# Second gate as eight columns, and half of one expert's w1 in the place that this frees

## The chip, the cores and the metric

The kernel runs on one core of a Trainium2 chip. The metric is the device time of one execution in microseconds (us). Before the change it is 517.47 us, the median of three runs (516.98 to 517.79).

A core has five engines that run side by side, each through its own instructions in order: TensorE (PE in the profile; the loading of its stationary operand is PEld), VectorE (DVE), ScalarE (ACT), GpSimd (POOL) and SyncE (SP). All large loads are issued by SP, in one queue. 16 DMA engines move the data.

## The reference

One decoder layer over 256 tokens of 1024 features: a token mixer (retention and latent attention), and then a mixture of 32 experts in 4 groups, of which each token uses two of one group. Before both halves a vector `c` is turned by `w_ada` into shifts, scales and gates. What matters here is the last part and the second gate `g2`:

```
mod = silu(c) @ w_ada + b_ada
sh1, sc1, g1, sh2, sc2, g2 = split(mod, 6)
...
u = rmsnorm(h, norm2) * (1 + sc2) + sh2
h = h + g2 * hier_moe(u)          # 32 experts: (silu(u w1) * (u w3)) w2, weighted by the router
return rmsnorm(h, final_norm)
```

`w1` and `w3` of an expert are 1024 x 256 and `w2` is 256 x 1024, all float32: 1 MiB each, 96 MiB for the experts.

## The kernel before

The token mixer fills the first 300 us. Then comes the router (line 1426 on), and after it eight batches of four experts, batch `bt` with the experts 4 bt to 4 bt + 3. An expert takes at most 32 tokens, so the four experts of a batch make 128 rows. A batch is

- `hidden`: w1 and then w3 of its four experts, 64 + 64 products of 32 x 256 (`hidden_mm`, line 1418; w1 and w3 have 8 blocks k of 128 rows each),
- `gather` for the next batch: one-hot rows pick the tokens (line 1358), and four and four transposes (line 1369) turn them into `ug`,
- `expert_out`: w2 (line 1532), times the gate `g2b` (line 1535), and the sum into four accumulators (line 1541).

**Slots.** On-chip memory is cut into 27 slots of 128 partitions x 2048 floats, 1 MiB each (`Slots`). A load of a weight takes a whole slot, whatever it loads into it. Work tiles take slots as well: `ad["g"]` (the slot s20) holds, in its first half, first the gate g1 and later the gathered tokens `ug`, and in its second half `g2b`; `y` is the slot of batch results, taken after batch 0's `hidden`.

**Order of the loads.** `Loads` holds a fixed list: per batch four w1, four w3, four w2. Whenever a slot is taken or given back, `pump` issues the next loads of the list, as long as slots are free and a plan, made in a first dry pass, says that the work tiles will still find theirs. A slot that comes free goes to the end of a queue of free slots. On SP the loads then stand in that order, and each waits there for the last reader of what was in its slot; a load that waits holds up all loads behind it. In batch 0 w1 and w3 are loaded in quarters over four experts (`QB`), so that their eight slots come free one after the other as the products go on; in the other batches the four w1 slots come free together, then the four w3 slots and, at the end of `expert_out`, the four w2 slots.

**The second gate.** During the mixer VectorE adds up the products of `silu(c)` and the last sixth of `w_ada`, so that `g2b` holds partial sums per partition (part 5 of `ada2_task`). In the router `rows_of` (line 1043) sums them over the partitions and spreads the sum over all partitions in one step, in two halves: a product of a matrix of ones with 512 columns (line 1047), and a copy by ScalarE back into the same place (line 1048). The order of PE and DVE in the router is written out by hand; after it a scheduler orders the instructions of each engine.

Of the kernel before, what the change touches and what calls it, by code (L numbers as in the profile page):

```python
# [13 lines left out]
AF = mybir.ActivationFunctionType  # L14
# [16 lines left out]
QB = ("w1", 0), ("w3", 0), ("w3", 7)  # L31
# [21 lines left out]
FIRST = 4  # L53
RES_AT = 1
OVER_AT = 3

PACE_AT, PACE = 19, 2

# [149 lines left out]
def body(ctx, tc, A, out, plan=None):  # L208
    nc = tc.nc
    T, V, S, G, Q = nc.tensor, nc.vector, nc.scalar, nc.gpsimd, nc.sync  # L210
# [3 lines left out]
    SL = Slots(sp, NSLOT, 2048, "s")  # L214
    PB = Slots(pp, 8, 512, "b")
    LD = Loads(SL, plan)
    ring = Ring(SL)

    def bank(name="bank"):
        return PB.alloc(name)  # L220
# [26 lines left out]
    def ld(view, src):  # L247
        def fn(t):
            n = 1
            for d in src.shape[1:]:  # L250
                n *= d
            Q.dma_start(t[:, :n].rearrange(view[0], **view[1]) if view else t[:, :n], src)  # L252
        return fn

    def ld_k(src):

        return ld(("p (k n) -> p k n", dict(k=src.shape[1])), src)
# [43 lines left out]
    def ew(name, e):  # L301
        g, i = divmod(e, 8)
        k = 8 if name != "w2" else 2
        return A[name][0, g, i].rearrange("(p k) n -> p k n", k=k)
# [12 lines left out]
    def ld_quarter(name, b, kp):  # L317

        src = A[name][0, b // 2, b % 2 * 4:b % 2 * 4 + 4].rearrange("e (p c k) n -> p e c (k n)", c=4, k=2)
        return ld(("p (e n) -> p e n", dict(e=4)), src[:, :, kp])  # L320
# [5 lines left out]
    for b in range(8):  # L326
        for name in ("w1", "w3"):
            for j in range(4):
                LD.add((name, 4 * b + j), ld_quarter(name, b, j) if (name, b) in QB else ld_k(ew(name, 4 * b + j)))
            if (name, b) == ("w1", 7):  # L330
                LD.add("fn", ld_fn)
        for j in range(4):
            if b < 7:
                LD.add(("w2", 4 * b + j), ld_k(ew("w2", 4 * b + j)))
# [4 lines left out]
    cols2 = st.tile([128, 8], F32, name="n2c")  # L339
# [3 lines left out]
    ident = cst[:, C_ID:C_ID + 128]  # L343
    one = st.tile([128, 1], F32, name="one")
# [40 lines left out]
    def keep_warm(n, after=None):  # L385

        pb = bank()
        with tc.issue_after(after) if after is not None else ExitStack():
            for _ in range(n):
                T.matmul(pb.t, onesb, oneb[:, 0:1].to_broadcast([128, 512]), start=True, stop=True)  # L390
        pb.free()
# [83 lines left out]
    start = ExitStack()  # L475
# [4 lines left out]
    pb = bank()  # L480
# [7 lines left out]
    pb = bank()  # L488
# [155 lines left out]
    ad = {"g": SL.alloc("g12")}  # L644
# [398 lines left out]
    def rows_of(a, o, ns=range(2)):  # L1043

        for n in ns:
            pb = bank()
            T.matmul(pb.t, ones, a[:, n * 512:(n + 1) * 512], start=True, stop=True)
            S.activation(o[:, n * 512:(n + 1) * 512], pb.t, AF.Copy)
            pb.free()
# [144 lines left out]
    for i, u in enumerate(units):  # L1194
# [13 lines left out]
        if i + LOOK < len(units):  # L1208
            units[i + LOOK].prep()
            j, r = divmod(i - (i_y - PACE_AT), PACE)  # L1210
# [66 lines left out]
    def h_turned(b, w):  # L1277

        for i in range(8 // w):
            pb = bank()  # L1280
            for k in range(w):
                T.transpose(pb.t[:, k * 128:(k + 1) * 128], hp[:, b, w * i + k, :], ident)
            copy((V, S)[i % 2], ug[:, w * i:w * (i + 1), :], pb.t[:, :w * 128].rearrange("p (k t) -> p k t", k=w))
            pb.free()
# [48 lines left out]
    def ranks(b):  # L1333
        pb = bank()
        T.matmul(pb.t[:, 0:32], utri, Mb[:, b, :], start=True, stop=b == 0, skip_group_check=True)
        if b == 1:
            T.matmul(pb.t[:, 0:32], onesb, Mb[:, 0, :], start=False, stop=True, skip_group_check=True)
        V.scalar_tensor_tensor(rk1[:, b, :], pb.t[:, 0:32], 1.0, Mb[:, b, :], op0=ALU.add, op1=ALU.mult)
        pb.free()
# [3 lines left out]
    Sr = sml.rearrange("p (b s) -> p b s", b=2)  # L1343
    GT = rt_t.rearrange("p b n -> p (b n)")
    ht = wr.rearrange("p k n -> p (k n)")[:, 0:256]
    g2b = ad["g"].t[:, 1024:2048]
    ug = ad["g"].t[:, 0:1024].rearrange("p (k s) -> p k s", k=8)
    iota = cst[:, C_IOTA:C_IOTA + 32]

    def onehot(bt, b):  # L1350
        e4 = slice(4 * bt, 4 * bt + 4)
        V.tensor_tensor(S01[:, b], iota[:, None, :].to_broadcast([128, 4, 32]),
                        rk1[:, b, e4][:, :, None].to_broadcast([128, 4, 32]), ALU.is_equal)
        return V.tensor_scalar(Sr[:, b], S01[:, b].rearrange("p e s -> p (e s)"), rstd2[:, b:b + 1], None, op0=ALU.mult)  # L1354
# [42 lines left out]
    def gather(bt):  # L1397
        pg = [bank() for _ in range(2)]
        for b in range(2):
            onehot(bt, b)  # L1400
            gather_mm(pg, b)
        gather_out(pg, y_s.t[:, 1024:2048])
# [3 lines left out]
    def hidden_mm(bt, m, ks):  # L1406

        name = ("w1", "w3")[m]
        ph = ph_of[m]
        cut = (name, bt) in QB  # L1410
        for k in ks:
            c = k // 2 if cut else 0
            for j in range(4):
                if cut:
                    w = LD.get((name, 4 * bt + c)).t.rearrange("p (e k n) -> p e k n", e=4, k=2)[:, j, k % 2, :]
                else:
                    w = LD.get((name, 4 * bt + j)).t.rearrange("p (k n) -> p k n", k=8)[:, k, :]
                i = T.matmul(ph.t[32 * j:32 * j + 32, 0:256], ug[:, k, 32 * j:32 * j + 32], w,  # L1418
                             start=k == 0, stop=k == 7, skip_group_check=True, tile_position=(0, 32 * j))
            if cut and k % 2:  # L1420
                LD.done((name, 4 * bt + c))
            if cut and bt == 7 and k % 2:
                keep_warm(WARM7[m], i.ins)
        return i

    router = ExitStack()
    router.enter_context(tc.manual_schedule(engines={T.engine, V.engine}))
# [11 lines left out]
    hl_act["m"][1].free()  # L1439
    h_of(1)  # L1440
    ranks(0)
    rows_of(g2b, g2b, (0,))
    h_turned(1, 2)
    onehot(0, 0)
    h_rstd(1)
# [5 lines left out]
    keep_warm(WARM2)  # L1451
    ranks(1)
    onehot(0, 1)
    rows_of(g2b, g2b, (1,))
    keep_warm(WARM3)
    first_mm(pg, 1, range(FIRST))
    first_out(pg, range(FIRST))
    hidden_mm(0, 0, range(2))
    first_mm(pg, 1, range(FIRST, 8))
    last_v = first_out(pg, range(FIRST, 8)).ins  # L1460
# [6 lines left out]
    def combine_weights(bt):  # L1467
        e4 = slice(4 * bt, 4 * bt + 4)
        pb = bank()
        for b in range(2):  # L1470
            V.tensor_tensor(S01[:, b], S01[:, b], Gt[:, b, e4][:, :, None].to_broadcast([128, 4, 32]), ALU.mult)
            T.transpose(pb.t[:, b * 128:(b + 1) * 128], S01[:, b].rearrange("p e s -> p (e s)"), ident)
        S.activation(GT, pb.t[:, 0:256], AF.Copy)
        pb.free()
# [51 lines left out]
    def expert_out(bt, hdT):  # L1526
        py = [bank() for _ in range(2)]
        ts = [LD.get(("w2", 4 * bt + j)).t.rearrange("p (k n) -> p k n", k=2) for j in range(4)]
        for n in range(2):
            for k in range(2):  # L1530
                for j in range(4):
                    T.matmul(py[n].t[32 * j:32 * j + 32, :], hdT[:, k, 32 * j:32 * j + 32],  # L1532
                             ts[j][:, k, n * 512:(n + 1) * 512], start=k == 0, stop=k == 1, skip_group_check=True,
                             tile_position=(0, 32 * j))
            V.tensor_mul(y[:, n * 512:(n + 1) * 512], py[n].t, g2b[:, n * 512:(n + 1) * 512])
            py[n].free()
        for j in range(4):
            LD.done(("w2", 4 * bt + j))
        for b in range(2):
            for n in range(2):  # L1540
                T.matmul(fin[2 * b + n].t, GT[:, b * 128:(b + 1) * 128], y[:, n * 512:(n + 1) * 512], start=bt == 0,  # L1541
                         stop=bt == 7, skip_group_check=True)
# [61 lines left out]
    for bt in range(8):  # L1604
        if bt:
            combine_weights(bt)
        hdT = hidden(bt)
        if bt == 7:
            o_s = SL.alloc("out")
        if bt == 0:  # L1610
            fin = [bank("fin") for _ in range(4)]
            y_s = SL.alloc("y")
            y = y_s.t[:, 0:1024]
        if bt < 7:
            gather(bt + 1)
            expert_out(bt, hdT)
        if bt == RES_AT:

            for b in range(2):
                for n in range(2):  # L1620
                    f = fin[2 * b + n].t.rearrange("p (q k) -> p k q", k=8)
                    V.tensor_add(f, f, hp[:, b, :, n * 64:(n + 1) * 64])
        if bt == OVER_AT:
            overflow()
# [108 lines left out]
```

## Time and profile before

| | |
|---|---|
| median of 3 runs | 517.47 us |
| the profiled execution | 517.75 us, of which the profile's span is 516.0 us |
| PE busy | 488.7 us (95% of the span) |
| DVE, ACT, POOL busy | 283.1, 198.1, 61.4 us |
| moved by DMA | 174.86 MB, mean 339 GB/s |
| granted clock of TensorE | 0.99 of full speed |

The span runs from the first to the last instruction; the execution takes 1.75 us more. Matmuls are pipelined, and the profile's busy time of PE is not PE at its peak. A product of plain float32 shows as two weight loads and two matmuls, a transpose as one of each. The rows of the trace stand in their own section below. In the chain of waits the profile follows, back from the end, what released each instruction; a step called DMA there is a stretch in which a load was what was waited for.

### The profile page before, as it was taken

How to read it: one execution, taken by the hardware profiler on the slowest of the kernel's cores; microseconds unless marked ns; L12 is line 12 of the kernel's file. 1: busy time of each engine (PE TensorE's matmuls, PEld its weight loads, DVE VectorE, ACT ScalarE, POOL GpSimd, SP SyncE). 2: the span in 40 equal slices, each digit the busy share in tenths (PEclk: the TensorE clock that was granted, in tenths of full speed). 3: DMA queues.
4: the chain of work that ended last, by engine and by line, in shares of the span. 5: the costliest groups of instructions: out<-in, count | busy, mean ns of one | idle time of the engine just before them, and what ended most of it. 6: DMA issues, size and time to landing. Idle time of an engine off the chain costs nothing.

```text
span 516.0 us, 8592 instructions
## 1 busy us (share of the span) xinstructions
PE 488.7 (95%) x3432; PEld 339.0 (66%) x3435; DVE 283.1 (55%) x529; ACT 198.1 (38%) x366; POOL 61.4 (12%) x58
## 2 busy tenths in 40 slices
PE   6999999999999999999999999999999898969894
PEld 2778999997787878888888887443544434323332
DVE  2555789884696996984777746424333131302113
ACT  2545783453678444456534424202112020202013
POOL 1000321411000002105862000000000000000000
PEclk8999999999999999999999999999999999989998
DMA  9999999788967692899698898999999999999993
GB/s 270 324 318 358 314 339 399 304 305 309 358 229 267 207 362 84 304 373 382 243 370 325 313 360 293 417 406 422 415 420 418 415 422 415 419 421 417 393 330 113
DMA packets 68099, 174.86 MB, mean 339 GB/s; under 512 B 5423, under 2 KB 27092, under 8 KB 57817
## 3 DMA queue, kind: packets, MB, share of 16 engines
q1 hardware_dynamic: 65602, 174.01, 90.5%
q10 hardware_dynamic: 2454, 0.27, 0.4%
q8 instruction: 28, 0.46, 0.4%
q14 instruction: 15, 0.11, 0.1%
HBM read 173.22 MB, written 1.05 MB: 338 GB/s over the span
## 4 chain that ended last, share of the span: by engine, by line
PE 58%; DMA 27%; SPq 6%; DVE 4%; ACT 1%; issue 1%; POOL 1%; ACTq 1%; DVEq 0%; POOLq 0%
DMA s<-in_w 24%; PE b L381 10%; PE b L383 10%; PE b L382 10%; PE b L1418 5%; SPq L252 4%; SPq L244 2%; PE b L1532 2%; DMA s<-in_w_in 1%; PE b L1541 1%; PE b L1358 1%; PE b L535 1%; PE b L533 1%; PE b L534 1%; DVE s L467 1%
## 5 line engine op out<-in xcount | busy, mean ns | idle before, releaser
L467 DVE TENSOR_TENSOR s<-s,s 128x1024 fp32r<-128x1024 f32 (+2 forms) x92 | 103.5, 1136 | 43.9 <-ACT s L466 43.4
L466 ACT ACTIVATE s<-s 128x1024 fp32r<-128x1024 f32 (+2 forms) x92 | 83.5, 923 | 83.1 <-PE b L383 54.3
L381 PE MATMUL b<-s,s 128*128 128x512 f32 (+2 forms) x258 | 102.2, 396 | 1.0 <-ACT s L466 0.9
L383 PE MATMUL b<-s,s 128*128 128x512 f32 (+2 forms) x258 | 98.7, 383 | 0.0
L382 PE MATMUL b<-s,s 128*128 128x512 f32 (+2 forms) x258 | 98.1, 380 | 0.0
L1418 PE MATMUL b<-s,s 128*32 128x256 f32 x1024 | 62.3, 381 | 10.8 <-DMA s<-in_w 8.8
L381 PEld LDWEIGHTS b<-s,s 128*128 128x128 f32 x258 | 48.5, 188 | 15.6 <-ACT s L466 4.3
L1418 PEld LDWEIGHTS b<-s,s 128*32 128x32 f32 x1024 | 32.8, 110 | 38.5 <-DMA s<-in_w 11.9
L383 PEld LDWEIGHTS b<-s,s 128*128 128x128 f32 x258 | 48.4, 188 | 9.6 <-DVE s L467 0.4
L382 PEld LDWEIGHTS b<-s,s 128*128 128x128 f32 x258 | 48.6, 188 | 8.5 <-issue 0.2
L1064 DVE SCALAR_TENSOR_TENSOR s<-s,cs,s 128x1024 f32<-128x1024 f32 x32 | 41.4, 1292 | 0.3
L535 PE MATMUL b<-s,s 128*128 128x256 f32 x128 | 36.2, 284 | 0.4 <-DVE s L467 0.4
L533 PE MATMUL b<-s,s 128*128 128x256 f32 x128 | 36.4, 285 | 0.0
L534 PE MATMUL b<-s,s 128*128 128x256 f32 x128 | 36.2, 283 | 0.0
L1532 PE MATMUL b<-s,wr 128*32 128x512 f32 x224 | 34.1, 596 | 0.0
L377 DVE COPY s<-b 128x512 f32<-128x512 f32 (+2 forms) x13 | 8.1, 624 | 41.7 <-PE b L1358 29.0
L1358 PE MATMUL b<-s,sml 128*128 128x512 f32 x56 | 28.4, 639 | 0.2 <-DVE sml L1354 0.2
L375 ACT ACTIVATE s<-b 128x512 f32<-128x512 f32 (+2 forms) x25 | 14.1, 567 | 32.9 <-PE b L1358 18.3
L1541 PE MATMUL b<-s,rt 128*128 128x512 f32 x56 | 26.2, 611 | 0.0
L535 PEld LDWEIGHTS b<-s,s 128*128 128x128 f32 x128 | 24.4, 191 | 0.6 <-DVE s L467 0.6
L534 PEld LDWEIGHTS b<-s,s 128*128 128x128 f32 x128 | 24.4, 191 | 0.0
L533 PEld LDWEIGHTS b<-s,s 128*128 128x128 f32 x128 | 24.4, 191 | 0.0
(258 smaller groups left out, 631.6 us busy)
## 6 DMA issues: line engine op xcount, KB each, us to landing
s<-in_w SPq DMA_DIRECT2D x92, 1024.0 KB
s<-in_w_in SPq DMA_DIRECT2D x22, 1024.0 KB
s<-in_w_ada SPq DMA_DIRECT2D x16, 1024.0 KB
s<-in_w_ada SPq DMA_DIRECT2D x16, 512.0 KB
s<-in_w_mla_o SPq DMA_DIRECT2D x4, 1024.0 KB
s<-in_w_ret_o SPq DMA_DIRECT2D x4, 1024.0 KB
s<-in_w_out SPq DMA_DIRECT2D x4, 1024.0 KB
s<-in_w SPq DMA_DIRECT2D x6, 512.0 KB
```

The source lines that it names most:

```text
L381: T.matmul(o, l[0], r[0], start=start, stop=False, skip_group_check=True)
L382: T.matmul(o, l[1], r[0], start=False, stop=False, skip_group_check=True)
L383: return T.matmul(o, l[0], r[1], start=False, stop=stop, skip_group_check=True)
L466: S.activation(hi, src, AF.Copy)
L467: V.tensor_tensor(lo, src, hi, ALU.subtract)
L533: T.matmul(o, hi[:, f], mh, start=k == 0 and c == 0, stop=False, skip_group_check=True)
L534: T.matmul(o, hi[:, f], ml, start=False, stop=False, skip_group_check=True)
L535: T.matmul(o, lo[:, f], mh, start=False, stop=k == 7, skip_group_check=True)
L1064: V.scalar_tensor_tensor(a, t[:, kk, :], cs[:, k:k + 1], a, op0=ALU.mult, op1=ALU.add)
L1358: T.matmul(pg[k4].t, Sr[:, b], hp[:, b, 4 * k4:4 * k4 + 4, :].rearrange("p k q -> p (k q)"), start=b == 0, stop=b == 1, skip_group_check=True)
L1418: i = T.matmul(ph.t[32 * j:32 * j + 32, 0:256], ug[:, k, 32 * j:32 * j + 32], w, start=k == 0, stop=k == 7, skip_group_check=True, tile_po ...
L1532: T.matmul(py[n].t[32 * j:32 * j + 32, :], hdT[:, k, 32 * j:32 * j + 32], ts[j][:, k, n * 512:(n + 1) * 512], start=k == 0, stop=k == 1, s ...
```

## The change

Three edits:

- In the router `rows_of` is replaced by `g2_cols`: for each block k a product whose stationary operand is every eighth column of the partial sums (128 x 128) and whose moving operand is one column of ones. That gives g2 as 8 columns, which stand in `cols2`, a tile of 8 columns (in the trace n2c) whose earlier content is no longer read.
- The second half of s20 is then free. One load is added behind the second `g2_cols`: blocks 0 to 3 of w1 of expert 9 (`HALF`). The load of that expert's w1 in the list keeps its place and its slot, but loads only blocks 4 to 7.
- After `hidden` of batch 0 a new slot `g2` is taken, and `g2_rows` fills it: for each block k a product of column k, repeated 128 times as the stationary operand, with the identity, and after each four of them a ScalarE copy that writes with a stride of 8 floats. `expert_out` then reads `g2b` there as before, until the end.

```diff
+HALF = 9
@@ the list of loads
-                LD.add((name, 4 * b + j), ld_quarter(name, b, j) if (name, b) in QB else ld_k(ew(name, 4 * b + j)))
+                half = (name, 4 * b + j) == ("w1", HALF)
+                LD.add((name, 4 * b + j), ld_quarter(name, b, j) if (name, b) in QB else
+                       ld_k(ew(name, 4 * b + j)[:, 4 * half:, :]))
@@
-    g2b = ad["g"].t[:, 1024:2048]
+    gh = ad["g"].t[:, 1024:2048]
+    g2c = cols2
@@ hidden_mm
+                elif (name, 4 * bt + j) == ("w1", HALF):
+                    w = (LD.get((name, HALF)).t if k > 3 else gh).rearrange("p (k n) -> p k n", n=256)[:, k % 4, :]
@@
+    def g2_cols(ks):
+        pb = bank()
+        for k in ks:
+            T.matmul(pb.t[:, k:k + 1], gh[:, k::8], one, start=k == ks[0], stop=k == ks[-1], skip_group_check=True)
+        S.activation(g2c[:, ks[0]:ks[-1] + 1], pb.t[:, ks[0]:ks[-1] + 1], AF.Copy)
+        pb.free()
+
+    def g2_rows():
+        g = SL.alloc("g2").t[:, 0:1024]
+        for h in range(2):
+            pb = bank()
+            for k in range(4):
+                T.matmul(pb.t[:, k * 128:(k + 1) * 128], g2c[:, 4 * h + k:4 * h + k + 1].to_broadcast([128, 128]), ident,
+                         start=k == 0, stop=k == 3, skip_group_check=True)
+            S.activation(g.rearrange("p (q k) -> p k q", k=8)[:, 4 * h:4 * h + 4, :],
+                         pb.t.rearrange("p (k q) -> p k q", k=4), AF.Copy)
+            pb.free()
+        return g
@@ router
-    rows_of(g2b, g2b, (0,))
+    g2_cols(range(4))
...
-    rows_of(g2b, g2b, (1,))
+    g2_cols(range(4, 8))
+    Q.dma_start(gh.rearrange("p (k n) -> p k n", k=4), ew("w1", HALF)[:, 0:4, :])
@@ batch loop, bt == 0, after hidden(0) and the slot for y
+            g2b = g2_rows()
```

The queue of SP, from the first w1 of batch 2 on. A row is a load; behind the arrow is the weight, before it the slot and the number of the tile. 128x2048 is a whole slot, 128x1024 half of one. Before:

```order
L252 DMA s10_2863<-in_w1 128x2048
L252 DMA s25_2958<-in_w1 128x2048
L252 DMA s15_2979<-in_w1 128x2048
L252 DMA s0_2989<-in_w1 128x2048
L252 DMA s1_2999<-in_w3 128x2048
L252 DMA s3_3011<-in_w3 128x2048
L252 DMA s18_3021<-in_w3 128x2048
L252 DMA s13_3031<-in_w3 128x2048
L252 DMA s5_3138<-in_w2 128x2048
L252 DMA s22_3140<-in_w2 128x2048
```

and with the change:

```order
L254 DMA s10_2863<-in_w1 128x2048
L1483 DMA s20_664<-in_w1 128x1024
L254 DMA s25_2965<-in_w1 128x1024
L254 DMA s15_2986<-in_w1 128x2048
L254 DMA s0_2996<-in_w1 128x2048
L254 DMA s1_3006<-in_w3 128x2048
L254 DMA s3_3018<-in_w3 128x2048
L254 DMA s18_3028<-in_w3 128x2048
L254 DMA s5_3156<-in_w3 128x2048
L254 DMA s22_3158<-in_w2 128x2048
```

The slots s25, s15, s0 and s1 held w1 of batch 0, s3, s18, s13 and s11 its w3, and s5, s22, s21 and s6 its w2. The fourth w3 of batch 2 has moved from s13 to s5, and every load behind it has moved by one slot too: s13 is now the slot of `y`, and s11, which was that of `y`, holds the new `g2`.

On PE, between `hidden` of batch 0 and `expert_out` (n2c is the tile of the 8 columns, cst holds the identity, sml the one-hot rows, s26 the tokens). Before:

```order
L1472 MATMUL b4_3072<-cst_64,S01_2760 128x128 x2
L1519 MATMUL b5_3079<-cst_64,wr_79 128x128 x2
L1358 MATMUL b3_3088<-s26_2376,sml_89 128x512
L1358 MATMUL b4_3089<-s26_2376,sml_89 128x512
L1358 MATMUL b3_3088<-s26_2376,sml_89 128x512
L1358 MATMUL b4_3089<-s26_2376,sml_89 128x512
L1369 MATMUL b1_3100<-cst_64,s11_3087 128x128 x4
L1532 MATMUL b3_3118<-s5_2494,wr_79 32x512
```

and with the change:

```order
L1501 MATMUL b4_3077<-cst_64,S01_2760 128x128 x2
L1548 MATMUL b5_3084<-cst_64,wr_79 128x128 x2
L1447 MATMUL b3_3094<-cst_64,n2c_78 128x128 x4
L1447 MATMUL b4_3100<-cst_64,n2c_78 128x128 x4
L1363 MATMUL b1_3106<-s26_2376,sml_89 128x512
L1363 MATMUL b5_3107<-s26_2376,sml_89 128x512
L1363 MATMUL b1_3106<-s26_2376,sml_89 128x512
L1363 MATMUL b5_3107<-s26_2376,sml_89 128x512
L1374 MATMUL b3_3118<-cst_64,s13_3092 128x128 x4
L1561 MATMUL b1_3136<-s5_2494,wr_79 32x512
```

The eight products of `g2_rows` stand ahead of the gather of batch 1, and so ahead of the products with w2 (s5 is the first of its slots).

## Rows read from the trace of the kernel before

**Rows 1.** The page: busy time by engine, and GB/s in 40 slices.
```profile
PE 488.7 (95%) x3432; PEld 339.0 (66%) x3435; DVE 283.1 (55%) x529; ACT 198.1 (38%) x366; POOL 61.4 (12%) x58
...
GB/s 270 324 318 358 314 339 399 304 305 309 358 229 267 207 362 84 304 373 382 243 370 325 313 360 293 417 406 422 415 420 418 415 422 415 419 421 417 393 330 113
```

**Rows 2.** Chain of waits, last third: start us, us, what was waited for.
```profile
365.90 19.29 DMA s<-in_w
...
462.73 21.35 DMA s<-in_w
...
496.59 8.02 DMA s<-in_w
```

**Rows 3.** Stages: us, busy time by engine, PE clock, DMA share, GB/s.
```profile
318.00:320.00 2.00, 2.00 (x26) 1.30 (x24) 0.82 (x2) 1.35 (x3) 0.00 (x0) 1.00 0.49 197
320.00:322.00 2.00, 2.00 (x31) 1.53 (x32) 1.19 (x8) 1.18 (x4) 0.00 (x0) 1.00 0.40 82
322.00:338.00 16.00, 15.61 (x155) 7.12 (x148) 7.55 (x37) 4.16 (x14) 0.00 (x0) 1.00 1.01 418
338.00:342.00 4.00, 4.00 (x18) 1.63 (x22) 0.96 (x3) 0.10 (x1) 0.00 (x0) 1.00 0.99 379
342.00:482.00 140.00, 130.27 (x1134) 57.29 (x1126) 37.08 (x94) 21.63 (x49) 0.00 (x0) 0.99 1.01 418
```

**Rows 4.** Timeline of SP's queue, single issues: start us, us, what.
```profile
320.08 0.33 SPq L252 DMA_DIRECT2D s<-in_w  x1
...
322.17 0.33 SPq L252 DMA_DIRECT2D s<-in_w  x1
...
326.48 0.33 SPq L252 DMA_DIRECT2D s<-in_w  x1
...
337.10 0.33 SPq L252 DMA_DIRECT2D s<-in_w  x1
...
345.40 0.33 SPq L252 DMA_DIRECT2D s<-in_w  x1
```

**Rows 5.** What SP waited for, at 320.08 and at 337.10: us, times, longest.
```profile
SPq L252 <- PE b L1418: 8.7, 1, 8.7
...
SPq L252 <- PE b L1532: 10.2, 1, 10.2
```

**Rows 6.** Chain of waits in the router and batch 0.
```profile
305.91 1.71 PE b L1289 x16
...
310.51 0.95 PE b L1047 x2
...
312.34 2.09 PE b L1289 x16
314.43 1.86 PE b L1383 x16
...
316.79 1.12 PE b L1047 x2
...
328.58 3.70 PE b L1358 x8
```

**Rows 7.** Timeline, ACT in the router, then PE after batch 0's hidden.
```profile
312.00 0.57 ACT L1048 ACTIVATE s<-b 128x512 f32<-128x512 f32 x1
...
327.83 0.51 PE L1519 MATMUL b<-cst,wr 128*128 128x128 f32 x2 [0.16 <-DVE wr L1515]
```

**Rows 8.** Lines with strided and plain operands: duration ns min/median/max.
```profile
L1519 PEld LDWEIGHTS b<-cst,wr x16: 194/196/223, 327.8 to 497.3; 128*128 128x128 f32 x16
L1472 PEld LDWEIGHTS b<-cst,S x16: 138/140/143, 327.2 to 473.7; 128*128 128x128 f32 x16
L1075 PE MATMUL b<-s,one x16: 623/632/639, 128.2 to 160.4; 128*32 128x256 f32 x16
L1418 PE MATMUL b<-s,s x1024: 379/379/403, 318.9 to 495.6; 128*32 128x256 f32 x171
L1202 ACT ACTIVATE s<-s x2: 2180/2194/2207, 241.8 to 243.9; 128x1024 f32<-128x1024 f32 x2
```

## The prediction

> **What bounds the kernel now.** I read the page first: PE is busy for 95% of the span [rows 1], which says little, since matmuls are pipelined. The row of GB/s says more: it goes up and down between 84 and 399 until slice 25 and stands between 406 and 422 from slice 26 to 37, that is from about 322 us to within 40 us of the end. The chain of waits bears it out: from 365.90 us on it is made of long stretches of DMA, the last from 496.59 to 504.61 [rows 2]. So from some point on the expert weights set the end, and what matters is when that flow starts, and whether it ever stops. The reader is to find both in the table of stages [rows 3]: 197 and 82 GB/s in the two stages from 318 to 322, then 418 for 16 us, 379 in 338 to 342, and 418 again for 140 us. A load of 1 MiB is 1.0486 MB, which at 418 GB/s takes 2.51 us.
>
> Then SP's queue tells why the flow starts where it does. At 320.08 a load goes out that had waited 8.7 us for a product of hidden, line 1418 [rows 4, 5]: until then all slots were full, and DMA ran dry. From 320.08 to 326.48 there are seven issues, one for each quarter of w1 and w3 of batch 0 that comes free (the eighth slot becomes y). The next issue is at 337.10, after 10.2 us of waiting for a product with w2, line 1532 [rows 4, 5]: the first w2 slot of batch 0. So DMA has seven loads to live on between 320 and 337. Did they last? The stage 320 to 322 moved 0.16 MB, worth 0.4 us at the full rate, so I count the flow as begun at 321.6, 1.5 us after the issue. Seven loads end at 321.6 + 7 x 2.51 = 339.2. The issue at 337.10 flows from 338.6. It just lasted, with 0.6 us to spare; the stage 338 to 342 at 379 instead of 418 GB/s [rows 3] is a loss of 0.16 MB or 0.4 us at that seam. This seam is where the change acts.
>
> **The loads, step by step.** The order of SP's queue shows that the change has two effects on this stock. Half a load, 0.52 MB, goes out ahead, when PE is through with the second g2_cols, near 318; it flows in the gap that stages 318 to 322 show, where 2 us x (418 - 197) + 2 us x (418 - 82) = 1.1 MB of room was left. That is worth 0.52 / 0.418 = 1.25 us. But the load of w1 of expert 9 still takes a whole slot for its other half, and g2 takes one more for good. So between 320 and the first w2 slot only six loads are issued, one of them half: 5.5 loads in place of 7. The fourth w3 of batch 2, the seventh load before, now stands behind the wait for the w2 slot s5.
>
> Before, that w3 began to flow at 321.6 + 6 x 2.51 = 336.7. With the change it cannot begin before the issue at 337.10 plus 1.5 us, plus whatever PE is late by then. The stock itself is gone earlier: the second load behind the new one cannot be issued before 322.17 [rows 4], so it flows from 323.7, and five whole loads end at 336.2, all of it moved by PE's delay in the router. Between the end of the stock and the restart DMA stands still. From that w3 on the bytes are the same in both kernels, so the end moves by the difference of its two starts.
>
> **What PE is late by, in the router (d).** Each half of rows_of was 0.95 and 1.12 us on PE [rows 6]. Each g2_cols has four products, thus eight weight loads of 128 x 128, and the loads bind, since one moving column is next to nothing. At the plain rate 16 such loads took 1.71 us in the logits, line 1289 [rows 6], 107 ns each, so 0.86 us for eight. But every eighth column is a read with a stride of 32 bytes. No row has such a weight load. The nearest two: a transpose whose stationary operand has a stride of two floats (line 1519) has weight loads of 196 ns, where plain ones (line 1472) have 140; and a product whose moving operand has a stride of eight floats (line 1075) lasts 632 ns, where the same shape unstrided (line 1418) lasts 379 [rows 8]. So 56 ns more for 128 columns is one end, and 253 ns for 256 columns, 127 ns for 128, the other. A load is then 163 to 234 ns, and a half 1.3 to 1.9 us. I take 200 ns, 1.6 us: the second row has the right stride but is no weight load. That adds 0.65 and 0.5 us, 1.15 in all. [...]
>
> ScalarE gives something back. Its copy of 0.57 us at 312.00 [rows 7] stood ahead of the evictions of the turned tokens, for which the second logits waited: 2.09 us against 1.71 for the first [rows 6]. The copy of 128 x 4 in its place is short, so up to 0.38 us returns. d = 1.15 - 0.38, about 0.8 us. Bounds: with plain loads (0.86 - 0.95) + (0.86 - 1.12) - 0.38 = -0.7, of which the one-hot rows of VectorE, for which the next product waits anyway, let me keep -0.6; with 234 ns and nothing given back 0.9 + 0.8 = 1.7.
>
> **In batch 0 (e).** g2_rows is eight products of 128 x 128 by 128 columns, the same kind as line 1383, of which 16 records took 1.86 us [rows 6]. They stand between the transposes of line 1519, which begin at 327.83 and last 0.51 us [rows 7], and the gather at 328.58 [rows 6], so 0.24 us of them falls into idle time: e = 1.6, less some overlap with the transposes, 1.5 us. Bounds 1.4 and 1.9. Its two copies on ScalarE write 512 floats with a stride of eight; 1024 read with that stride took 2.19 us [rows 8], so 1.1 us each at most. They are over by 331.5, a microsecond before the gather of this kernel has its first result to copy out, and long before line 1535 needs g2b; I put them at nothing. Without that cover they would cost what of these 2.2 us the gather has to wait.
>
> The rest costs nothing: hidden of batch 2 reads two places instead of one, more than 30 us after both halves have landed. The slot lost is lost in later batches too, but there frees run ahead of DMA: behind the four w2 slots the next four come free at 345.40 [rows 4], here 347.7, 1.5 us later flowing, while their four loads last from 340.9 to 350.9.
>
> **The sum.** Restart 337.10 + d 0.8 + e 1.5 + 1.5 = 340.9 us, against 336.7: 4.2 us. The 0.4 us lost at the seam before is not lost a second time: 3.8 us. The profiled execution took 517.75 us (span 516.0 and 1.75 around it), so the changed one would take 521.5; the median of the runs is 0.28 lower, and that gives **521.3 us**. With the lower bounds it is -0.6 + 1.4 + 1.9 - 0.4 = 2.3 us or 519.8, with the upper ones and nothing back from the seam 1.7 + 1.9 + 1.9 = 5.5 us or 523.0.
>
> **Rivals.** *Strided weight loads cost nothing.* Then d is -0.6 and, with e 1.5, the shift is 2.4 us: 519.9. For it: no row shows a weight load with a stride of eight floats, and the loads of line 1289 go at 107 ns with PE otherwise idle, so there may be room for a slower read. Against it: line 1519. [...]
>
> *The half load is a pure gain.* If the stock lasts, the gap of 318 to 322 takes in 0.52 MB, nothing else changes, and the end comes 1.25 us sooner: 516.2. It decides where the first w2 slot is free before the stock ends: 5.5 loads from 321.6 end at 335.4, so the issue would have to stand at 333.9 or earlier. For it: the gap is real, and the flow then sets the end. Against it: that issue is at 337.10 [rows 4] even without g2_rows in front.
>
> *No change.* If the end hung on PE, or DMA had slack later, the hole would be made good: 517.5. For it: PE's 95%. Against it: 140 us at 418 GB/s without a dent [rows 3], and PE waiting for DMA at the end [rows 2].
>
> *A stride costs four times.* With 430 ns a load each g2_cols takes 3.4 us, d is near 4.5, and the end comes at 525. For it: nothing but the lack of a row; against it: line 1075.
>
> **How the numbers follow.** Forecast 0.64, free strides 0.16, pure gain 0.07, no change 0.05, dear strides 0.08. The forecast's own range is 519.8 to 523.0; free strides lie in it or just below, so 519.3 to 523.5 leaves out the last three, 2 in 10. About 0.2%, or 1 us, can be told from no change. Faster is the pure gain, 0.07; within 0.2% is no change, 0.05; slower is all else, 0.88.
>
> **What would show it.** In the changed kernel's stages there is a hole of some 3 to 4 us near 337 to 341 us in which DMA moves next to nothing, and the rate of 418 from there to the end; the half load shows as flow near 320. The issue that waits for line 1561 (1532 before) stands near 339.4, with the half load in s20, the half load in s25 and five whole ones ahead of it. The weight loads of g2_cols show 200 ns apart; 107 would be the first rival. A flow without a hole, or a second hole near 348, would make the forecast wrong.

## The result and the profile after

| | before | after |
|---|---|---|
| median, us (range, runs) | 517.54 (516.98 to 518.05, 6) | 522.51 (521.30 to 526.64, 6) |
| after / before | | 1.0106, 95% interval 1.0079 to 1.0133 |
| the profiled execution, us | 517.75 (span 516.0) | 524.48 (span 522.8) |
| granted clock of TensorE, mean | 0.99 | 0.986 |

The change costs 5.0 us at the median, 1.2 us more than forecast, and the range held it. The six times stand apart: 521.30, 521.44 and 521.62, then 523.40, 524.48 and 526.64. The profiled execution is one of the long ones. So its rows hold the forecast's terms and something more. The median lies in the gap between 521.62 and 523.40: with one more long execution among the six it would have been 523.4 or more, above the upper bound of the forecast's sum, 523.0. That the range held is in part luck.

The page first: PE's busy time, the granted clock in 40 slices, GB/s in the same slices. It answers to [rows 1].

```profile
PE 497.7 (95%) x3460; PEld 347.2 (66%) x3463; DVE 283.4 (54%) x529; ACT 199.6 (38%) x368; POOL 61.5 (12%) x58
...
PEclk9999999999999999999999997999999998999998
...
GB/s 274 322 321 363 287 360 399 283 337 309 309 235 249 267 325 79 361 392 261 312 408 328 313 341 199 370 321 418 418 421 418 416 418 419 418 421 418 396 347 126
```

Three slices differ in kind, the 25th to the 27th (314 to 353 us): 199, 370 and 321 where [rows 1] have 293, 417 and 406, and the 25th has a 7 in the row of the clock. From the 28th on the flow is as before. The stages, which answer to [rows 3], show two holes:

```profile
318.00:320.00 2.00, 2.00 (x9) 1.66 (x10) 0.09 (x1) 0.00 (x0) 0.00 (x0) 0.50 0.21 86
320.00:322.00 2.00, 1.78 (x10) 1.61 (x9) 0.77 (x3) 0.00 (x0) 0.00 (x0) 0.86 0.00 0
322.00:338.00 16.00, 15.84 (x178) 10.27 (x178) 6.63 (x38) 6.59 (x17) 0.00 (x0) 1.00 0.82 298
338.00:342.00 4.00, 4.00 (x28) 1.52 (x31) 1.92 (x4) 1.90 (x5) 0.00 (x0) 1.00 0.84 354
342.00:346.00 4.00, 4.00 (x23) 1.35 (x16) 1.70 (x3) 0.00 (x0) 0.00 (x0) 1.00 0.47 166
346.00:482.00 136.00, 127.73 (x1122) 56.42 (x1121) 35.97 (x92) 21.41 (x48) 0.00 (x0) 0.99 1.01 418
```

The second hole, 166 GB/s in 342 to 346, is the one forecast. The first, about 322 us, is the old gap before the first w1 slot, grown longer. Behind 346 us there is none. SP's queue, single issues, beside [rows 4] (L1483 is the half load into s20, the next is the half into s25; at 343.10 goes the load that waits for the first w2 slot of batch 0, called the w2 issue below):

```profile
322.64 0.33 SPq L1483 DMA_DIRECT2D s<-in_w  x1
...
324.80 0.33 SPq L254 DMA_DIRECT2D s<-in_w  x1
...
326.88 0.33 SPq L254 DMA_DIRECT2D s<-in_w  x1
...
343.10 0.33 SPq L254 DMA_DIRECT2D s<-in_w  x1
...
351.41 0.33 SPq L254 DMA_DIRECT2D s<-in_w  x1
```

And what SP waited for in 330 to 345 us, beside [rows 5]: line 1561 is the product with w2, 1532 before.

```profile
SPq L254 <- PE b L1561: 11.7, 2, 11.5
```

The queue is the one forecast: half a load, half a load, five whole ones, then the wait for the products with w2. The two halves, 0.52 MB each, go out 2.16 us apart, which is at most 243 GB/s: a part of why 322 to 338 us moves only 298. The w2 issue stands at 343.10 instead of 337.10, 6.0 us later. Why is read from the chain of waits in the router and in batch 0, beside [rows 6]: start, length, what.

```profile
310.31 1.88 PE b L1437 x8
...
313.12 2.95 PE b L1293 x16
316.07 3.57 PE b L1388 x16
...
320.55 2.05 PE b L1437 x8
...
323.73 1.00 PE b L1425 x16
...
333.05 1.79 PE b L1447 x16
334.84 3.44 PE b L1363 x8
```

In the chain of before, the first products with w1 (line 1418, now 1425) start here:

```profile
319.02 1.00 PE b L1418 x16
```

So PE comes out of the router 323.73 - 319.02 = 4.7 us late, and the gather of batch 1 starts 334.84 - 328.58 = 6.26 us late, 1.55 us of it from `g2_rows` (line 1447). The gather itself is 0.26 us shorter, 3.44 for 3.70, which leaves the 6.0 us. Of the 4.7 us the strided products explain 1.7: 1.88 + 2.05 instead of 0.95 + 1.12 for the two halves of `rows_of` is 1.86, less 0.19 that ScalarE gave back (line 1293 takes 1.90 us for 2.09 where the clock stays up). The router starts 0.2 us sooner here (310.31 for 310.51). Most of the rest stands in lines 1293 and 1388, which the change does not touch. They take 2.95 and 3.57 us, and 1.90 and 1.86 in a profile in which the clock did not fall (experiment 3). Stages of the same execution, with the granted clock as third number from the end:

```profile
312.00:313.00 1.00, 1.00 (x9) 0.88 (x9) 0.42 (x1) 0.78 (x4) 0.00 (x0) 1.00 1.01 410
313.00:314.00 1.00, 1.00 (x10) 0.96 (x8) 0.96 (x4) 0.60 (x3) 0.00 (x0) 0.87 0.96 303
314.00:316.00 2.00, 2.00 (x11) 2.00 (x11) 0.07 (x1) 0.00 (x0) 0.56 (x1) 0.50 1.01 406
316.00:318.00 2.00, 2.00 (x11) 2.00 (x11) 1.61 (x11) 0.00 (x0) 0.00 (x0) 0.50 0.98 410
```

and of before:

```profile
314.00:316.00 2.00, 2.00 (x19) 2.00 (x19) 1.28 (x9) 0.00 (x0) 0.00 (x0) 1.00 0.91 356
316.00:318.00 2.00, 1.93 (x10) 1.03 (x10) 1.19 (x7) 0.05 (x1) 0.00 (x0) 1.00 1.04 434
```

From 314 to 320 us the granted clock is 0.50, with PE busy throughout; before it stood at 1.00 here. That is a cost of about 3 us in this execution, which no rival of the prediction held.

The terms of the forecast therefore come out like this:

| term, us | forecast | measured |
|---|---|---|
| d (PE late in the router), full clock | 0.8 | 1.6 from the span's start, 1.7 from the start of the first `g2_cols` (experiment 6) |
| d, this execution | 0.8 | 4.7 |
| e (`g2_rows` in batch 0) | 1.5 | 1.55 |
| spacing of the strided loads, ns | 200 | 235 (1.88 us / 8) |

### The profile page after: what moved, and what is told of

Same layout as the page of the kernel before. It is cut to its first block, busy times and chain, and to the rows that moved or that the text cites. A ratio compares the mean times of both kernels' runs of the same rounds, so it can differ in the third digit from the quotient of the medians.

```text
span 522.8 us, 8652 instructions
## 1 busy us (share of the span) xinstructions
PE 497.7 (95%) x3460; PEld 347.2 (66%) x3463; DVE 283.4 (54%) x529; ACT 199.6 (38%) x368; POOL 61.5 (12%) x58
## 3 DMA queue, kind: packets, MB, share of 16 engines
HBM read 173.22 MB, written 1.05 MB: 333 GB/s over the span
## 4 chain that ended last, share of the span: by engine, by line
PE 54%; DMA 32%; SPq 6%; DVE 4%; POOL 1%; ACT 1%; issue 1%; ACTq 0%; DVEq 0%; POOLq 0%
DMA s<-in_w 29%; PE b L385 10%; PE b L387 10%; PE b L386 10%; SPq L254 4%; PE b L1425 2%; DMA s<-in_w_in 2%; SPq L246 2%; PE b L1561 2%; PE b L1570 1%; PE b L539 1%; PE b L537 1%; PE b L538 1%; PE b L1388 1%; DVE s L471 1%; DMA s<-in_w_ada 1%
## 5 line engine op out<-in xcount | busy, mean ns | idle before, releaser
L1425 PE MATMUL b<-s,s 128*32 128x256 f32 x1016 | 64.4, 389 | 9.1 <-DMA s<-in_w 9.1
L385 PEld LDWEIGHTS b<-s,s 128*128 128x128 f32 x258 | 48.5, 188 | 14.6 <-ACT s L470 3.3
L387 PEld LDWEIGHTS b<-s,s 128*128 128x128 f32 x258 | 48.4, 188 | 9.3
L386 PEld LDWEIGHTS b<-s,s 128*128 128x128 f32 x258 | 48.6, 188 | 8.4 <-issue 0.2
L1561 PE MATMUL b<-s,wr 128*32 128x512 f32 x224 | 35.5, 596 | 0.4 <-DMA s<-in_w 0.4
L1363 PE MATMUL b<-s,sml 128*128 128x512 f32 x56 | 26.6, 604 | 0.0
L539 PEld LDWEIGHTS b<-s,s 128*128 128x128 f32 x128 | 24.4, 191 | 0.6 <-DVE s L471 0.6
L538 PEld LDWEIGHTS b<-s,s 128*128 128x128 f32 x128 | 24.5, 191 | 0.0
```

What stands on the lines that cost most here:

```text
L385: T.matmul(o, l[0], r[0], start=start, stop=False, skip_group_check=True)
L386: T.matmul(o, l[1], r[0], start=False, stop=False, skip_group_check=True)
L387: return T.matmul(o, l[0], r[1], start=False, stop=stop, skip_group_check=True)
L538: T.matmul(o, hi[:, f], ml, start=False, stop=False, skip_group_check=True)
L539: T.matmul(o, lo[:, f], mh, start=False, stop=k == 7, skip_group_check=True)
```

## The experiments

Each was timed in five rounds beside the kernel before: experiments 1 to 4 in one set (before 517.24), 5 and 6 in the next (517.46, with 7 and 8), 9 and 10 in the last (517.20).

**1. The slot alone.** Before, and a slot that nobody uses, taken behind y in batch 0.

```diff
+            SL.alloc("idle")
```

> The kernel before with one slot more taken after y in batch 0 and never used; nothing else is changed. Slot theory: the fourth w3 of batch 2 has to wait for the first w2 slot of batch 0, so it flows from 337.1 + 1.5 = 338.6 us instead of 336.7, and 0.4 us of the seam of before is not lost again: +1.5 us, 519.0, with a hole of about 2 us in the flow near 337 to 339. Rival (the loss of the change is the PE work that it adds, and the slot has no part in it): 517.5, no hole.

Measured: 518.50 us (518.14 to 520.14, 12 runs), ratio 1.0027 (1.0016 to 1.0039). The stages:

```profile
336.00:338.00 2.00, 2.00 (x16) 0.54 (x8) 1.18 (x3) 0.00 (x0) 0.00 (x0) 1.00 0.45 152
338.00:340.00 2.00, 2.00 (x6) 0.71 (x5) 0.52 (x1) 0.00 (x0) 0.00 (x0) 1.00 0.85 262
```

PE does nothing else than before, and the w2 issue stands at 336.93. Yet the stock of loads is gone before that, and a hole of 2 x (418 - 152) + 2 x (418 - 262) = 0.84 MB opens, 2.0 us of flow; before already lost 0.4 us at this seam [rows 3]. That is 1.6, and the time rose by 1.3 (518.50 - 517.24). One slot taken for good costs about what the forecast's working gives for it: 1.9 us (338.6 against 336.7) less 0.4, that is 1.5.

**2. Without the half load.** The change, with all of w1 of expert 9 in its slot.

```diff
-HALF = 9
+HALF = -1
-    Q.dma_start(gh.rearrange("p (k n) -> p k n", k=4), ew("w1", HALF)[:, 0:4, :])
```

> The changed kernel without the half load: w1 of expert 9 is loaded whole into its slot, the freed half of s20 stays empty. Slot theory: that w3's start hangs on the restart after the hole and not on what flowed before, so the time is that of the change: 521.4 where TensorE's clock stays up in the router, up to 524.5 where it falls. Rival (the half load earns its 1.25 us and the loss is elsewhere): 1.25 us slower than the change, 522.7 and more.

Measured: 523.04 us (521.38 to 524.49, 4 runs), ratio 1.0119 (1.0094 to 1.0144), like the change with the half load. The median alone would fit the rival too (522.7 and more); the fastest run, 0.1 us from the change's, does not, and neither does the trace. In the profiled execution (521.38) the clock did not fall, and the w2 issue stands here:

```profile
339.94 0.33 SPq L254 DMA_DIRECT2D s<-in_w  x1
```

From there to the end of the span it takes 179.7 us, and in the change 179.7 too (522.8 - 343.10). The early half MB buys nothing that can be told, as the stock runs out with and without it.

**3. No stride.** The change, but the columns are made from plain blocks of 128, and `g2_rows` writes without a stride.

```diff
-            T.matmul(pb.t[:, k:k + 1], gh[:, k::8], one, ...)
+            T.matmul(pb.t[:, k:k + 1], gh[:, k * 128:(k + 1) * 128], one, ...)
-            S.activation(g.rearrange("p (q k) -> p k q", k=8)[:, 4 * h:4 * h + 4, :],
-                         pb.t.rearrange("p (k q) -> p k q", k=4), AF.Copy)
+            S.activation(g[:, 512 * h:512 * h + 512], pb.t, AF.Copy)
```

> The changed kernel with the eight columns taken from eight blocks of 128 neighbouring columns instead of every eighth one, and the rows written back without a stride. Stride theory: a weight load goes back from 235 to 107 ns, each g2_cols from 1.9 to 0.9 us, the first w2 slot comes free about 2 us sooner than with the change: 519.5 to 520.2. And if it is the length of this thin stretch that lets the clock fall, no execution lies above 521. Rival (the clock falls because one-column products follow one another, whatever their stride): some executions 2 to 5 us above the others still.

Measured: 519.70 us (519.16 to 520.96, 7 runs), ratio 1.0038 (1.0003 to 1.0074). The chain in the router:

```profile
310.77 0.88 PE b L1437 x8
...
312.58 1.90 PE b L1293 x16
314.48 1.86 PE b L1388 x16
316.84 1.05 PE b L1437 x8
...
319.02 1.00 PE b L1425 x16
```

Eight loads take 0.88 us, 110 ns each, and line 1425 starts at 319.02, as in before: d is 0, or -0.3 counted from the start of the first `g2_cols`, which stands at 310.77 here for 310.51. What is left is the slot and `g2_rows`. Against experiment 1 that is 1.2 us for e, against the change 2.8 us for the stride and what comes with it. The same line in both kernels, duration min/median/max, this one first and the change second:

```profile
L1437 PEld LDWEIGHTS b<-one,s x16: 186/192/200, 310.6 to 317.6; 128*128 128x128 f32 x16
```

```profile
L1437 PEld LDWEIGHTS b<-one,s x16: 312/335/337, 310.1 to 322.2; 128*128 128x128 f32 x16
```

The record of such a load lasts longer than the spacing of two of them: 192 ns at a spacing of 110, 335 at 235. It is the spacing that sums up on PE here, 0.88 and 1.88 us for eight loads.

**4. Filler products.** The change, with three products of 512 columns (of the kind the kernel uses to keep PE busy, line 394) behind the first `g2_cols`.

```diff
     g2_cols(range(4))
+    keep_warm(3)
```

> The changed kernel with three filler products of 512 columns (0.22 us each) behind the first g2_cols. Clock theory: the 0.5 granted from 314 to 320 us in the profiled execution is what parts the executions at 523 to 527 from those at 521.4; with the filler the clock holds, and all lie near 521.4 + 0.6 = 522. Rival (the spread comes from the DMA hole, or from elsewhere): a spread of 4 us or more stays, and the clock falls as before.

Measured: 523.62 us (522.17 to 524.16, 4 runs), ratio 1.0114 (1.0088 to 1.0140). The stages:

```profile
320.00:321.00 1.00, 1.00 (x8) 0.97 (x9) 0.00 (x0) 0.27 (x2) 0.00 (x0) 1.00 0.08 16
321.00:322.00 1.00, 1.00 (x9) 0.75 (x12) 0.46 (x2) 0.82 (x2) 0.00 (x0) 0.54 0.45 94
322.00:323.00 1.00, 1.00 (x12) 0.40 (x8) 0.36 (x1) 0.00 (x0) 0.00 (x0) 0.50 0.88 274
```

The clock stayed at 1.00 behind the first `g2_cols` and fell behind the second, and nothing was won: not the expected 522. That the fillers moved the fall is not shown, as in experiment 5 it stands behind the second `g2_cols` without them.

**5. `g2_rows` behind the w2 products.** The change, with the eight products put behind the last product with w2 of batch 0.

```diff
+            with tc.issue_after(after):     # the last product with w2 of batch 0
                 for k in range(4):
                     T.matmul(pb.t[:, k * 128:(k + 1) * 128], g2c[...].to_broadcast([128, 128]), ident, ...)
```

> The changed kernel with g2_rows issued behind the products with w2 of batch 0 instead of ahead of the gather. Slot theory: the first w2 slot comes free 1.5 us sooner (e goes to nothing), the hole is 1.5 us shorter, and the end comes 1.5 us sooner than with the change: 519.9 where the clock holds in the router, about 521.5 to 523 where it falls. Rival (PE work in batch 0 is hidden behind the loads anyway): no gain, 521.4 and more.

Measured: 525.34 us (522.81 to 528.22, 6 runs), ratio 1.0142 (1.0098 to 1.0185): a miss, slower than the change by 1.5 us between the fastest runs. The chain behind the w2 products:

```profile
341.07 1.10 PE b L1450 x8
342.17 0.02 issue
342.19 2.03 ACT s L1452 x2
```

The w2 issue came earlier, at 340.28, in part because the clock fell for a shorter time, but now the two strided copies on ScalarE (2.03 us), which the gather had covered, stand in the chain. Hidden of batch 1 is late by them, its w1 slots with it, and there is a second hole:

```profile
352.00:354.00 2.00, 2.00 (x44) 1.23 (x40) 0.42 (x1) 0.39 (x1) 0.00 (x0) 1.00 0.56 164
```

From the w2 issue to the end of the span it takes 181.5 us for the change's 179.7. The work was not taken off the path; it was moved in front of the next free that DMA waits for. The clock fell as well in the profiled execution (0.50 in 320 to 323 us).

**6. The slot given back.** The change, with g2 in the half of expert 9's slot that the half load leaves unused, so that no slot more is taken in batch 0; that slot is then kept to the end.

```diff
-        g = SL.alloc("g2").t[:, 0:1024]
+        g = LD.get(("w1", HALF)).t[:, 1024:2048]
```

> The changed kernel with g2 written into the unused half of the slot of expert 9's w1, which is then kept to the end, so that no slot is taken in batch 0. Slot theory: the stock is 6.5 loads, the first load that waits for a w2 slot is w2 again; with the strided columns (1.6 us without a fall of the clock) and g2_rows (1.5 us) it starts at 341.7 instead of 339.2, and with the 0.4 us of the seam that is +2.1 us: 519.6, and up to 522.6 where the clock falls. Rival (the slot is not what costs): as the change, 521.4 and more.

Measured: 521.69 us (519.18 to 524.58, 12 runs), ratio 1.0076 (1.0052 to 1.0099). In the profiled execution (519.79) the clock did not fall; line 1425 starts 1.61 us after before's, and the w2 issue stands at 340.00:

```profile
310.38 1.88 PE b L1437 x8
...
320.63 1.00 PE b L1425 x16
```

From the first `g2_cols` to line 1425 that is 10.25 us, and in before 8.51 (319.02 - 310.51): 1.74 us more. The hole is a dip:

```profile
340.00:342.00 2.00, 2.00 (x9) 0.59 (x4) 0.83 (x2) 0.00 (x0) 0.00 (x0) 1.00 0.87 258
```

Between this median and the change's lie 0.8 us, between the fastest runs 2.1; experiment 1 had 1.3 for the slot. The long executions blur it.

**7 and 8. All three mended.** Plain blocks, late `g2_rows`, no extra slot; 8 also gives the half load to expert 11, the last w1 of batch 2, so that the load into the first slot that comes free is whole.

```diff
-HALF = 9
+HALF = 11
```

> All three cures in the changed kernel: columns from blocks of 128, g2_rows behind the products with w2, g2 in the free half of expert 9's slot. Slot theory: nothing is late, the stock of 6.5 loads begins flowing whole at 323.7 and lasts to 338.8, and the w2 load starts there instead of at 339.2; with up to 0.4 us of the seam that is 0.4 to 0.8 us sooner than before: 516.5 to 516.9. Rival (something else in the change costs, as the load in s20 that stands in SP's queue): not below 517.3.

> As the kernel with all three cures, but the w1 that is loaded in two halves is that of expert 11, the last of batch 2, and not that of expert 9, the second. The load into the first slot that comes free is then whole, and covers the time to the next issue at 322.17. Slot theory: the stock ends at 321.6 + 6.5 x 2.51 = 337.9, the w2 load starts at the restart, 338.6, 0.6 us sooner than before: 516.5 to 516.9, at most 0.2 us better than with expert 9. Rival: the early half is worth its whole 1.25 us once the first load is whole: 516.0.

Measured: 518.28 (517.52 to 522.25, 12 runs), ratio 1.0009 (0.9987 to 1.0031), and 517.45 (516.38 to 518.85, 12 runs), ratio 0.9986 (0.9967 to 1.0005). Both missed the expected 516.5 to 516.9. What the change loses is won back, in experiment 7 all but 0.8 us, and nothing more. The traces show two places where flow is lost. One stands behind the late `g2_rows`: hidden of batch 1 starts at 344.0 us in both instead of 341.80, the first load into its w1 slots goes out at 347.6 instead of 345.40, and the rate dips. Experiment 7, and then before:

```profile
348.00:350.00 2.00, 2.00 (x45) 1.19 (x39) 0.42 (x1) 0.16 (x1) 0.00 (x0) 1.00 1.02 348
```

```profile
348.00:350.00 2.00, 2.00 (x21) 1.01 (x14) 0.42 (x1) 0.00 (x0) 0.00 (x0) 1.00 1.00 414
```

From 348 to 354 us experiment 7 moves 0.34 MB less than before and experiment 8 0.25 MB, worth 0.8 and 0.6 us at 418 GB/s. That the late loads bring the dip is argued only, as the DMA engines stay busy in it (share 1.02). The other place is the early half load. Where the half MB went is seen in the stages of experiment 8:

```profile
318.00:320.00 2.00, 2.00 (x26) 1.30 (x25) 0.82 (x2) 0.94 (x3) 0.00 (x0) 1.00 1.02 360
320.00:322.00 2.00, 2.00 (x28) 1.51 (x32) 1.27 (x8) 1.26 (x5) 0.00 (x0) 1.00 0.76 242
322.00:324.00 2.00, 2.00 (x44) 1.17 (x36) 1.92 (x17) 0.68 (x6) 0.00 (x0) 1.00 0.93 315
324.00:326.00 2.00, 2.00 (x44) 1.22 (x40) 0.85 (x4) 0.21 (x1) 0.00 (x0) 1.00 0.79 238
```

against these of before:

```profile
322.00:324.00 2.00, 2.00 (x44) 1.23 (x40) 1.92 (x18) 0.68 (x7) 0.00 (x0) 1.00 1.01 426
324.00:326.00 2.00, 2.00 (x44) 1.17 (x36) 0.93 (x5) 0.28 (x1) 0.00 (x0) 1.00 0.98 385
```

With before's 197 and 82 [rows 3] for the first four, the early load brings 2 x (360 - 197) + 2 x (242 - 82) = 0.65 MB into the gap, and the next 4 us move 2 x (426 - 315) + 2 x (385 - 238) = 0.52 MB less. In 318 to 328 as a whole it is 311 GB/s for 303, or 0.08 MB. The DMA engines are busy (share 0.76 to 1.02) at a low rate; why, these runs don't tell.

**9. Plain loads twice.** Experiment 3 with every product of `g2_cols` done twice, to part the stride from the length of the stretch (each product then starts and stops its own sum).

```diff
-        for k in ks:
+        for k in [k for k in ks for _ in range(2)]:
```

> The kernel e3_plain with every one-column product of g2_cols done twice, the second over the first: sixteen plain weight loads a half in place of eight, so that the stretch on TensorE is about as long as with the strided loads (16 x 110 ns = 1.8 us against 1.88) without a stride. PE late by 0.9 + 0.7 us, as with strided loads at the full clock. Theory A (the length of a stretch in which TensorE only loads weights makes its granted clock fall): the clock falls to 0.5 behind the second g2_cols in some executions, and times run from 520.9 to 524 as those of the change do. Theory B (the strided reads make it fall): the clock stays near 1.00 in the profiled execution, times lie within 2 us of each other, and the median is e3_plain's 519.7 plus 1.0 to 1.6 us: 520.7 to 521.3.

Measured: 521.42 us (521.00 to 527.78, 12 runs), ratio 1.0092 (1.0061 to 1.0123). The stages of the profiled execution (523.26):

```profile
314.00:315.00 1.00, 1.00 (x11) 1.00 (x11) 0.41 (x2) 0.00 (x0) 0.51 (x1) 0.93 0.75 254
315.00:316.00 1.00, 1.00 (x6) 1.00 (x6) 0.20 (x1) 0.00 (x0) 0.04 (x1) 0.50 1.01 344
```

The clock falls to 0.50 without any stride. The theory that it takes a strided read to bring it down is refuted. The other one, that a long row of one-column products does, fits: experiment 3, with half the loads, kept 1.00. Each is one profile, so this is argued more than shown.

**10. The stride alone.** Experiment 8 with the columns read with the stride again.

```diff
-            T.matmul(pb.t[:, k:k + 1], gh[:, k * 128:(k + 1) * 128], one, ...)
+            T.matmul(pb.t[:, k:k + 1], gh[:, k::8], one, ...)
```

> The kernel e8_half11 with one thing put back: the columns of g2_cols are read with the stride of eight floats (the rows are still written without one, so the second gate comes out in another order). No slot is lost and g2_rows still comes late, so this prices the strided loads by themselves. PE is late by 1.6 us at the first w2 slot (issue near 338.6). Theory B (strides make the clock fall): some executions lose 3 us more, times spread over 3 us or more, median 518.5 to 521. Theory A (length alone): the same here, as the stretch is as long as in the change. Rival (only the sum of all edits brings the fall): times within 2 us of each other, 518.5 to 519.1.

`g2_rows` still writes without a stride here, so the second gate comes out in another order and the output is not the layer's; no instruction has another shape by that. Measured: 521.01 us (519.07 to 523.57, 10 runs), ratio 1.0070 (1.0035 to 1.0105). No slot is lost here and no `g2_rows` stands early, and still 3.6 us are lost against experiment 8, 2.7 between the fastest runs. Its profiled execution (519.15) is a short one, with the clock at 1.00 all through the router. Line 1425 starts at 320.92, 1.98 us after experiment 8's, and the w2 issue at 339.00 is 1.98 us after too: that is the stride. The rest lies in the long executions. So the fall doesn't come in every execution. That it comes without the other edits is not shown, as no trace of this kernel has it.

Over all runs: of the seven kernels with the long stretch (the change, experiments 2, 4, 5, 6, 9 and 10), 18 of 54 executions are more than 2.5 us above the fastest of their kernel; of the others (before in all its runs, each set by itself, experiments 1, 3, 7 and 8), 8 of 117. That the long ones are those in which the clock fell here is not shown. Of the four profiled executions with the fall only the change's is so long; those of experiments 4, 5 and 9 lie 1.6, 0.6 and 2.3 us above the fastest of their kernel. Of the other executions only the mean clock is known. It is lower in the long ones (experiment 10: 0.978 and 0.981 in the three longest, 0.993 and 0.997 in the two shortest), but it is also low in a long one of before, 523.14 us at 0.979, which has no such stretch.

## Why the prediction was right, point by point

- **The seam with the first w2 slot.** Right. The stock of loads, the order in the queue and the hole came as worked out, and a slot alone opens that hole (experiment 1: 1.3 us for 1.5). With PE later than forecast, the hole stands near 341 to 345 us instead of 337 to 341, and the w2 issue at 343.10 instead of 339.4. The rivals "pure gain" and "no change" fell.
- **The half load earns nothing.** Right: experiment 2 is no slower than the change beyond the spread, and lasts as long behind its w2 issue. One sign failed: the half load did not flow near 320 us in the profiled execution, but was issued at 322.64, behind the late router.
- **e, `g2_rows` in batch 0.** 1.55 us for 1.5. That the copies are hidden was right too, and experiment 5 showed what they cost without that cover.
- **d, PE late in the router.** This is the term that was mis-sized: 1.6 for 0.8 at the full clock, or 1.7 counted from the start of the first `g2_cols` (1.74 in experiment 6, 1.75 in experiment 10), which is its upper bound. The two stretches take 3.94 us for the forecast's 3.2, and ScalarE gave back 0.19 us of the 0.38. Between the two nearest rows the prediction took the middle, 200 ns. Line 1075 alone, which has the stride of eight floats, was the better row to go by: 234 ns worked out, 235 measured, and 110 without the stride (experiment 3). Also, the 196 and 140 ns of [rows 8] are durations of records, and experiment 3 shows for its loads that the duration is not the spacing (192 ns for 110).
- **The rival "free strides".** Fell. It was priced at 519.9, and experiment 3, which really takes the strides away, came to 519.7.
- **The clock.** Missing altogether. With 1.3 (slot), 1.6 (d) and 1.5 (e) the sum is 4.4 us; the fastest runs of change and before are 4.3 apart (521.30 - 516.98), the medians 5.0. The rest is put down to the fall of the clock, which is seen in the profiled execution only: 3 us there, and 1.6 us in those of experiments 4 and 5 (lines 1388 and 1425 against experiment 6). By it the profiled execution comes near the d of the rival "a stride costs four times" (4.7 for 4.5 us), but for another reason: the loads are 235 ns apart and not 430.
- **From 6.0 us at the w2 issue to 6.7 in the time.** The long last waits for DMA agree with the end: 503.31 in the chain of after, 496.59 in [rows 2], 6.72 apart. By the forecast's own working, 6.0 and the 1.9 of the slot less 0.4 would be 7.5. The missing 0.8 lies behind the w2 issue: from there to the end of the span before takes 178.9 us, and the kernels that lose the slot (the change, experiments 1 to 4 and 9; experiment 5 has its second hole besides) take 179.6 to 179.9, so that the slot is worth 0.7 to 1.0 us by the profiles, for 1.5 forecast and 1.3 by the times of experiment 1. Why is open; there is one profile of before.

## What to carry to other kernels

Count the loads that are in stock between two frees, not the slots: here a slot taken for good cost time at the one seam where DMA already lived on its last load, 1.3 us of the 2.5 that a load takes. Price a strided operand by a row with the same stride first, even if it is of another instruction (here 234 ns for 235), and sum spacings rather than durations of records (here 110 ns for 192, and 235 for 335). Work that is moved off one wait can come to stand in front of the next one, as the 2.03 us of copies did in experiment 5, so look which cover it loses.

## What the runs showed of the hardware that was not expected

- The granted clock of TensorE fell to 0.50 behind rows of one-column products of some 1.9 us, for 3 to 6 us, in four of the seven profiled kernels with such rows (the change, experiments 4, 5 and 9), with PE busy at 1.00 by the profile when it fell. With rows of 0.88 and 1.05 us (experiment 3) it stayed at 1.00. Three filler products behind the first row didn't prevent the fall behind the second (experiment 4, 0.50 in 322 to 324 us). What decides in which executions it comes is open.
- The weight loads of 128 x 128 float32 with a stride of 32 bytes had a spacing of 235 ns (the change, 1.88 us for eight), the plain ones 110 (experiment 3, 0.88 us for eight).
- In experiment 8 a half load sent early flowed at 242 to 360 GB/s and the loads behind it at 238 to 315, where before had 385 to 426; the gap of 1.1 MB took in 0.08 MB net.
